# A decoder layer's down product as seven block products, with sums of weights in small chunks on GpSimd and norms on VectorE and ScalarE

## The chip, the cores and the metric

The kernel runs on one core of a Trainium2 chip. The metric is the device time of one execution in microseconds (us). A core has five engines that run side by side and meet through semaphores: TensorE (PE in the rows; PEld is its weight load), VectorE (DVE), ScalarE (ACT), GpSimd (POOL) and SyncE (SP), which here issues every DMA. Each engine takes its instructions strictly in order, and so does SP: a DMA whose semaphores are not there yet holds back all DMAs behind it.

## What is computed

One decoder layer in float32, sequence 1024, width 1024: a mixing layer (dilated attention and a convolution branch), a layer norm, a gated feed-forward network (FFN) of 2816 features, and a second layer norm. The change touches the second half:

```python
ALPHA = 2 ** 0.25
h = silu(x @ w_gate) * (x @ w_up)          # (1024, 2816)
out = layer_norm(ALPHA * x + h @ w_down)   # (1024, 1024)
```

## The kernel before

Every float32 product is three matmuls of rounded halves: `split` (L65, L66) makes a high part by a copy on ACT and a low part by a subtraction on DVE, and `three` pairs them as hi·hi, hi·lo, lo·hi. A matmul has 512 columns and 128 rows of weights. Splits of weights go to five slots of 128x1024.

The FFN runs 22 blocks of 128 features (loop `f`). Each holds seven products, of 12 matmuls each (four slices of the contraction by three), in this order, by the names in the code: B11 and T2 (banks `pa`, `pb`), B21 (again `pa`), T3 (`pd`), T1 (`pc`), T4 (again `pd`), B22 (again `pc`). It is a two-by-two block scheme with seven instead of eight products: the weight sums T1 to T4 are made on DVE (class `Weights`, steps `first` to `fifth`) from two raw units of 512 KB, gate `g` and up `u`, which SP fetches into a pool of three buffers. The next block's steps are written between this block's products. DVE takes each bank out of PSUM with an add (L984, L993, L998, L1000, L1007), since T4 adds onto the bank that T3's add has read. The finished `h` tile of 128x1024 is stored to DRAM (`hd`, L1011), one store per block. The first three blocks (`NEARLY`) have their B11 and B21 products earlier, ahead of the loop.

The down stage is the plain product. For each half `p` of the rows it runs over 22 feature blocks, and for each loads a weight unit (512 KB) and half an `h` tile (256 KB), splits both, and issues 4 row tiles x 2 column halves x 3 = 24 matmuls (L1081) into eight banks. The eight row tiles get `ALPHA * x` from ACT (L1074), then a norm: for seven of them `layer_norm_act`, which gives 640 of 1024 columns of two elementwise steps (L785, L786) to GpSimd and 384 to DVE; for the last one `layer_norm` on DVE, with statistics taken by `bn_stats` (L1056, L1057). Behind the last matmul stand both halves of that last row tile.

The Tile framework's scheduler puts each engine's instructions in order when the kernel is built, so that the order in the code isn't the order on an engine; pools give buffers round robin, and a load into a buffer waits for its last reader.

## Time and profile before

| what | us |
|---|---|
| time before, median of 3 runs | 1659.48 |
| the runs | 1657.36 to 1659.85 |
| the profiled execution's own time | 1657.62 |
| its span (first to last instruction) | 1655.8 |
| PE busy | 1631.6 |
| VectorE busy | 993.4 |
| ScalarE busy | 686.4 |
| GpSimd busy | 47.8 |

The page of the profile gives busy times per engine, then 40 slices of the span, the DMA queues, the chain of work that ended last, the costliest groups of instructions, and DMA issues. "L921 PE" is the engine PE at line 921. A row of a timeline gives start, duration, engine, line, operation, output and inputs by the program's names, shape, count, and in square brackets the idle time ahead of it with what ended it. In the chain of waits a row is one piece of the path that ended last: start, duration, engine and bank. The FFN loop ends at about 1401 us, the down stage's matmuls run from 1404 to 1643 us, and the tail behind them up to 1655.8.

### The profile page before, as it was taken

To read this page: it belongs to the slowest core of one execution; us is meant where nothing else is said; L and a number is where in the kernel's file an instruction comes from. 1 tells how busy PE (TensorE), PEld (TensorE's weight loads), DVE (VectorE), ACT (ScalarE), POOL (GpSimd) and SP (SyncE) were. 2 spreads that over 40 slices of the span, in tenths; PEclk is the share of its full clock that TensorE was granted. 3 is DMA by queue.
4 is the path that set the end of the run, shared out by engine and by line. 5 is a ranking of instruction groups with operands and counts; after the bars stand their busy time and mean duration, and the time that the engine had idled before them with its cause. 6 is when DMAs were issued, how large, how long until landed. Compare 5 with 4: busy or idle time off the path is not lost.

```text
span 1655.8 us, 21072 instructions
## 1 busy us (share of the span) xinstructions
PE 1631.6 (99%) x8146; PEld 1333.3 (81%) x8146; DVE 993.4 (60%) x1599; ACT 686.4 (41%) x1263; POOL 47.8 (3%) x30
## 2 busy tenths in 40 slices
...
GB/s 261 60 43 52 45 52 159 51 46 39 74 153 52 52 77 131 132 252 168 287 92 216 51 77 76 83 95 91 77 76 77 90 89 190 273 146 141 203 89 52
DMA packets 70457, 185.02 MB, mean 112 GB/s; under 512 B 11324, under 2 KB 14652, under 8 KB 70356
## 3 DMA queue, kind: packets, MB, share of 16 engines
...
q14 instruction: 37, 0.30, 0.1%
...
## 4 chain that ended last, share of the span: by engine, by line
PE 93%; DVE 4%; ACT 1%; DMA 1%; issue 1%; DVEq 0%; SPq 0%; ACTq 0%
PE mm L176 43%; PE mm L921 9%; PE s L921 7%; PE t L921 7%; PE mm L1081 5%; PE s L176 4%; PE t L1081 3%; PE s L1081 3%; PE s L414 2%; PE pv L921 2%; PE pv L460 2%; PE pv L1081 2%; PE t L434 1%; PE mm L304 1%; PE pv L176 1%
## 5 line engine op out<-in xcount | busy, mean ns | idle before, releaser
L65 ACT ACTIVATE wh<-raw 128x1024 fp32r<-128x1024 f32 (+1 forms) x206 | 206.5, 1003 | 366.9 <-PE mm L176 83.1
L66 DVE TENSOR_TENSOR wl<-raw,wh 128x1024 fp32r<-128x1024 f32 (+1 forms) x206 | 239.7, 1165 | 192.1 <-ACT wh L65 191.1
L176 PE MATMUL mm<-xh,wh 128*128 128x512 f32 x752 | 298.6, 397 | 0.0
L176 PE MATMUL mm<-xl,wh 128*128 128x512 f32 x752 | 293.2, 390 | 0.0
L176 PE MATMUL mm<-xh,wl 128*128 128x512 f32 x752 | 293.2, 390 | 0.0
L176 PEld LDWEIGHTS mm<-xh,wh 128*128 128x128 f32 x752 | 141.1, 188 | 39.3 <-issue 9.9
L176 PEld LDWEIGHTS mm<-xh,wl 128*128 128x128 f32 x752 | 141.2, 188 | 29.9
L176 PEld LDWEIGHTS mm<-xl,wh 128*128 128x128 f32 x752 | 141.2, 188 | 27.8
L504 DVE SCALAR_TENSOR_TENSOR acc<-u,cp,acc 128x1024 f32<-128x1024 f32 x120 | 153.8, 1282 | 3.3
L347 ACT ACTIVATE sw<-mm 32x512 f32<-32x512 f32 x192 | 113.2, 589 | 35.7 <-PE mm L176 17.3
L66 DVE TENSOR_TENSOR xl<-t,xl 128x512 fp32r<-128x512 f32 x44 | 30.2, 691 | 104.1 <-ACT xl L65 100.8
L176 PE MATMUL mm<-wh,xh 128*128 128x512 f32 x232 | 91.5, 394 | 0.0
L1081 PE MATMUL mm<-wh,xl 128*128 128x512 f32 x264 | 88.5, 389 | 2.4 <-ACT xl L65 2.4
L176 PE MATMUL mm<-wh,xl 128*128 128x512 f32 x232 | 90.4, 390 | 0.0
L176 PE MATMUL mm<-wl,xh 128*128 128x512 f32 x232 | 90.3, 389 | 0.0
L349 DVE TENSOR_TENSOR tcs<-mm,cosF 128x512 f32<-128x512 f32 x48 | 33.1, 690 | 86.0 <-ACT sw L347 82.7
L65 ACT ACTIVATE xl<-t 128x512 fp32r<-128x512 f32 x44 | 27.4, 628 | 122.3 <-PE t L1081 118.8
L378 DVE CUSTOM_DVE_ANT_0 pt<-s,m2t 128x256 f32<-128x256 f32 (+1 forms) x128 | 41.3, 378 | 35.4 <-PE s L414 35.4
L1081 PE MATMUL s<-wh,xl 128*128 128x512 f32 x176 | 61.8, 389 | 0.0
L380 ACT ACTIVATE pt<-pt,stp 128x64 f32<-128x64 f32 (+2 forms) x128 | 49.9, 392 | 27.1 <-DVE stp L378 26.9
L1081 PE MATMUL t<-wh,xl 128*128 128x512 f32 x176 | 60.8, 389 | 0.0
L1081 PEld LDWEIGHTS mm<-wh,xl 128*128 128x128 f32 x264 | 49.6, 188 | 13.1 <-ACT xl L65 2.8
...
## 6 DMA issues: line engine op xcount, KB each, us to landing
raw<-wst SPq DMA_DIRECT2D x165, 512.0 KB, 3.3
hd<-h SPq DMA_DIRECT2D x22, 512.0 KB, 2.6
t<-hd SPq DMA_DIRECT2D x44, 256.0 KB, 3.4
gd<-gt SPq DMA_DIRECT2D x16, 512.0 KB, 3.6
m<-gd SPq DMA_DIRECT2D x32, 256.0 KB, 5.1
...
m<-pvd SPq DMA_DIRECT2D x24, 256.0 KB, 4.7
pvd<-pvs SPq DMA_DIRECT2D x16, 256.0 KB, 2.0
```

The source lines that it names most:

```text
L65: act.activation(hi, src, AF.Copy)
L66: dve.tensor_sub(lo, src, hi.bitcast(F32))
L176: pe.matmul(ps, a, b, start=j == 0, stop=j == n - 1)
L347: act.activation(sw[32 * q:32 * q + 32, :], ps[32 * (q ^ 1):32 * (q ^ 1) + 32, :], AF.Copy)
L349: dve.tensor_mul(tcs, ps, cosF[:, cols])
L378: dve.tensor_tensor_reduce(out=pt, in0=s, in1=msk, scale=-0.125, scalar=BIG, op0=ALU.add, op1=ALU.min, accum_out=mneg)
L380: act.activation(pt, pt, AF.Exp, bias=mneg, scale=-1.0, accum_out=den)
L414: pe.matmul(o, q[rows, i * P:(i + 1) * P], keys(k, i)[rows], start=True, stop=True)
L460: pe.matmul(pv[64 * hh:64 * hh + 64, :], V[g, keys[kb]][:, hd * 64:hd * 64 + 64], pT[:, hh * nb + kb, :], start=kb == 0, stop=kb == nb - 1)
L504: dve.scalar_tensor_tensor(acc, u[:, j:j + S], cp[:, c, j:j + 1], acc, op0=ALU.mult, op1=ALU.add)
L921: pe.matmul(ps, a, b, start=start and n == 0, stop=stop and n == 11, skip_group_check=True)
L1081: pe.matmul(banks[i][c], a, b, start=f == 0 and j == 0, stop=f == NFF - 1 and j == 2)
```

## The change

The down product becomes a seven-product block scheme as well, as in the FFN. The 1024 rows of `h` are cut in two halves of 512 and its 2816 features in two halves of 11 blocks (`NK`); A11, A12 and A22 are blocks of `h` that are stored as they are, and S1 to S4 are sums of blocks that GpSimd makes in place after every second feature block (`down_sums`, four adds of 128x512, then four stores of 256 KB). The FFN takes its feature blocks in pairs k, k + 11 (`FFN_ORDER`), so that the blocks of a pair are at hand together. The sums of `w_down` are made during the FFN as well: `down_weights` takes 22 chunks of [128, 4, 256], two loads of 256 KB each into a pool called `stage`, four subtractions or adds of 128x256 on GpSimd, two stores of 256 KB to DRAM (`twd`); they are named `tw` in the rows of order. The down stage is then a list `DOWN` of seven products of 11 blocks x 4 row tiles x 3 matmuls, 924 matmuls in place of 1056. Each step loads two pieces of 256 KB into the two halves of one 1024 wide tile, splits it at once, and issues 12 matmuls; splits run two steps ahead, loads five further, and six splits of the last product are made earlier and kept in slots of their own. Row tiles 4 to 7 are finished and normed during P2, tiles 0 to 3 in P3, whose four row tiles run one after the other. Behind the last matmul stands one half of one row tile.

The norms leave GpSimd and become two 1024 wide operations on DVE, with the square sum on ACT; the last tile keeps `bn_stats`. Raw units of `u` get two buffers of their own (`up2`), so that `g` has the pool of three alone, and fetches run one unit further ahead. In the FFN `second` moves behind the T1 product, `third` behind T4, `fourth` behind the store of `h`. In the last FFN block the first loads and splits of the down stage take the place of the next block's weights. Whole FFN matmuls, their number and their banks stay as they are.

```diff
-NTAIL = 4
+NK = 11
+FFN_ORDER = [k + NK * c for k in range(NK) for c in range(2)]
...
 
     def fetch(upto):
         while state["raw"] < min(upto, n_units):
             u = state["raw"]
-            t = wraw.tile([P, 1024], F32, tag="raw", name="raw")
+            t = unit_pool[0](u).tile([P, 1024], F32, tag="raw", name="raw")
...
             split(u, *w)
             self.T3, self.T1 = slot_halves(w)
-            fetch(taken[0] + 3)
+            fetch(taken[0] + 4)
...
     p4 = ExitStack()
-    gt8 = p4.enter_context(tc.tile_pool(name="gt8", bufs=8, reuse_waits="tile"))
-    h3 = p4.enter_context(tc.tile_pool(name="h3", bufs=3, reuse_waits="tile"))
+    gt6 = p4.enter_context(tc.tile_pool(name="gt6", bufs=6, reuse_waits="tile"))
+    h4 = p4.enter_context(tc.tile_pool(name="h4", bufs=4, reuse_waits="tile"))
+    up2 = p4.enter_context(tc.tile_pool(name="up2", bufs=2, reuse_waits="tile"))
+    unit_pool[0] = lambda u: up2 if u >= first_pair and (u - first_pair) % 2 else wraw
 
...
+    def row_tile():
+        return h4.tile([P, S], F32, tag="h", name="h")
+
+    def spill_sums(k, u, v):
+
+        for name, src in (("S2", u[:, LEFT]), ("S3", u[:, RIGHT]), ("S4", v[:, LEFT]), ("S1", v[:, RIGHT])):
+            sp.dma_start(hd[name][k], src)
+
+    def down_sums(k, u, v):
+
+        eng = nc.gpsimd
+        eng.tensor_add(v[:, RIGHT], v[:, RIGHT], u[:, RIGHT])
+        eng.tensor_sub(u[:, RIGHT], u[:, LEFT], u[:, RIGHT])
+        eng.tensor_sub(u[:, LEFT], v[:, RIGHT], u[:, LEFT])
+        eng.tensor_sub(v[:, LEFT], v[:, LEFT], u[:, LEFT])
+        after.append(lambda: spill_sums(k, u, v))
+
+    def down_weights(k, e):
+
+        t = stage.tile([P, 4, 256], F32, tag="sp", name="tw")
+        cols = slice(e * 256, (e + 1) * 256)
+
+        def rows(src, n):
+            return src[n].rearrange("p (c x) -> p c x", c=2)[:, :, cols]
+
+        sp.dma_start(t[:, 0:2], rows(wst, n_units + k))
+        sp.dma_start(t[:, 2:4], rows(wst, n_units + NK + k))
+        b11, b12, b21, b22 = (t[:, n] for n in range(4))
+        eng = nc.gpsimd
+        eng.tensor_sub(b12, b22, b12)
+        eng.tensor_add(b11, b12, b11)
+        eng.tensor_sub(b21, b21, b11)
+        eng.tensor_sub(b22, b22, b11)
+
+        def spill():
+            sp.dma_start(rows(twd, k), t[:, 0:2])
+            sp.dma_start(rows(twd, NK + k), t[:, 2:4])
+        after.append(spill)
+
+    chunks = deque((k, e) for k in range(NK) for e in range(2))
+
+
+    DOWN = [("P1", "A11", (0, 0), 0, True), ("P6", "S2", (2, 0), 1, True), ("P7", "S3", (2, 1), 0, True),
+            ("P5", "S1", (3, 1), 1, True), ("P4", "A22", (3, 0), 0, False), ("P2", "A12", (1, 0), 0, True),
+            ("P3", "S4", (1, 1), 1, False)]
...
+    for j in range(len(DOWN)):
+        for k in range(NK):
+            if (j, k) not in seq:
...
+    def split_upto(key, ahead):
+        upto = min(seq.index(key) + 1 + ahead, len(seq))
+        while dpos[1] < upto:
+            j, k = seq[dpos[1]]
+            load_upto(dpos[1] + 1)
+            w = kept[k] if j == len(DOWN) - 1 and k < len(kept) else slot()
+            split(draw.pop((j, k)), *w)
+            dsplit[j, k] = w
+            dpos[1] += 1
+            load_upto(dpos[1] + 5)
...
     for f in range(NFF):
         last = f == NFF - 1
+        todo, after = after, []
+        for fn in todo:
+            fn()
+        if f >= NEARLY:
+            for _ in range(2 if f in (5, 9, 13) else 1):
+                if chunks:
+                    down_weights(*chunks.popleft())
         V_, W = W, Weights()
...
-        if nxt:
-            nxt.second()
         u3, sg2 = half_tile(), half_tile()
...
         dve.tensor_add(u3, u2, pd)
-        if nxt:
-            nxt.third()
...
+        if nxt:
+            nxt.second()
         product(pd, V_.T4, a22, start=False)
...
         if nxt:
-            nxt.fourth()
+            nxt.third()
         else:
...
+        k = FFN_ORDER[f] % NK
+        if f % 2 == 0:
+            sp.dma_start(hd["A11"][k], ht[:, LEFT])
+            hrows.append(ht)
+        else:
+            sp.dma_start(hd["A12"][k], ht[:, LEFT])
+            sp.dma_start(hd["A22"][k], ht[:, RIGHT])
+            down_sums(k, hrows.pop(), ht)
         if nxt:
+            nxt.fourth()
             nxt.fifth()
...
+    def norm(i):
+        y = yt[i // 4][:, i % 4]
         sc = sc2[:, i]
-        for c in range(2):
-            yc = y[:, c * HALF:(c + 1) * HALF]
-            if i < 7:
...
+        if i == 3:
+            layer_norm(y, bs2, mv2, sc, g2, b2, HALF, emit_rows(i))
+            return
+        nmu, ssq, v, sd, r, t = (sc[:, n:n + 1] for n in range(2, 8))
+        dve.tensor_scalar(nmu, sc[:, 0:1], sc[:, 1:2], -1.0 / D, op0=ALU.add, op1=ALU.mult)
+        act.activation(junk, y, AF.Square, bias=nmu, accum_out=ssq)
+        act.activation(sd, ssq, AF.Sqrt, bias=eps, scale=1.0 / D)
+        dve.scalar_tensor_tensor(y, y, nmu, g2, op0=ALU.add, op1=ALU.mult)
+        dve.tensor_scalar(v, ssq, 1.0 / D, LN_EPS, op0=ALU.mult, op1=ALU.add)
+        rsqrt_of(v, sd, r, t)
+        dve.scalar_tensor_tensor(y, y, r, b2, op0=ALU.mult, op1=ALU.add)
+        emit_rows(i)(slice(0, D))
...
+    def after_product(name, i, ps):
+        if name == "P1":
+            act.activation(u2(i), ps, AF.Copy)
+            scaled(i, 0, u2(i))
+        elif name == "P6":
+            dve.tensor_add(u2(i), u2(i), ps)
+        elif name == "P7":
+            dve.tensor_add(u3(i), u2(i), ps)
+            scaled(4 + i, 0, u2(i))
+            scaled(i, 1, u2(i))
+            scaled(4 + i, 1, u3(i))
+        elif name == "P5":
+            add_in(4 + i, 1, ps)
+        elif name == "P4":
+            add_in(4 + i, 0, ps)
+        elif name == "P2":
+            add_in(i, 0, ps)
         else:
...
+    def loads():
+        for i in (0, 1, 2, 3, 4, 5, 6, 7):
+            sp.dma_start(yt[i // 4][:, i % 4], yd[i])
+            yield
+        ln_rows(1, g2, b2)
+        yield
+
...
+    for j, (name, _, _, sset, first) in enumerate(DOWN):
+        if first:
+            banks[sset] = [bank(t) for t in sets[sset]]
+        last = j == len(DOWN) - 1
...
+                pe.matmul(banks[sset][i], a, b, start=first and k == 0 and m == 0,
+                          stop=k == NK - 1 and m == 2, skip_group_check=True)
+
+        if not last:
+            for k in range(NK):
+                split_upto((j, k), 2)
+                for i in range(4):
+                    step(i, k)
+                    if k == NK - 1:
+                        after_product(name, i, banks[sset][i])
+                if k % 2 == 0:
+                    next(fill, None)
+                if name == "P2" and k in (1, 3, 5, 7):
+                    norm(4 + k // 2)
...
             for i in range(4):
...
+                for k in range(NK):
+                    if i == 0:
+                        split_upto((j, k), min(2, NK - 1 - k))
+                    step(i, k)
+                after_product(name, i, banks[sset][i])
+                norm(i)
```

Order on SyncE before, at the ends of feature blocks 4 to 6: `hd` is the store of a block's `h`, `raw` the fetches of two units for later blocks.

```order
L1011 DMA hd4_99<-h_8623 128x1024 [waits DVE_49]
L77 DMA raw_8760<-wst 128x1024 [waits DMAHW7_49,DVE_49,Activation_49]
L77 DMA raw_8762<-wst 128x1024 [waits DMAHW5_49,DMAHW1_49,DVE_49]
L1011 DMA hd5_100<-h_8751 128x1024 [waits DVE_49]
L77 DMA raw_8888<-wst 128x1024 [waits DMAHW2_49,DVE_49,Activation_49]
L77 DMA raw_8890<-wst 128x1024 [waits DMAHW4_49,DMAHW0_49,DVE_49]
L1011 DMA hd6_101<-h_8879 128x1024 [waits DVE_49]
L77 DMA raw_9016<-wst 128x1024 [waits DMAHW5_49,DVE_49,Activation_49]
L77 DMA raw_9018<-wst 128x1024 [waits DMAHW7_49,DMAHW3_49,DVE_49]
```

One store and two fetches stand there per block, and nothing between them waits for GpSimd. After, SyncE in the same part of the FFN; `tw` rows are loads of chunks and `twd` rows their stores, `raw_8897` is a unit of `g` and `raw_8750` a unit of `u`, `hdA11_2` a store of `h`.

```order
L979 DMA tw_9621<-wst 128x2x256 [waits DMAHW4_49]
L978 DMA tw_9767<-wst 128x2x256 [waits DMAHW5_49,DMAHW0_49]
L988 DMA twd4_176<-tw_9484 256x1x256 [waits DMAHW6_49,DMAHW1_49,Pool_49]
L989 DMA twd15_187<-tw_9484 256x1x256 [waits DMAHW7_49,DMAHW2_49,Pool_49]
L988 DMA twd5_177<-tw_9621 256x1x256 [waits DMAHW3_49,Pool_49]
L81 DMA raw_8897<-wst 128x1024 [waits DVE_49,Activation_49]
L989 DMA twd16_188<-tw_9621 256x1x256 [waits DMAHW4_49,Pool_49]
L979 DMA tw_9767<-wst 128x2x256
L81 DMA raw_8750<-wst 128x1024 [waits DVE_49]
L1094 DMA hdA11_2_97<-h_8735 128x512 [waits DMAHW5_49,DVE_49]
L988 DMA twd5_177<-tw_9767 256x1x256 [waits DMAHW6_49,Pool_49]
L989 DMA twd16_188<-tw_9767 256x1x256 [waits DMAHW7_49,DMAHW3_49,Pool_49]
```

The fetches of `raw` now stand behind stores that wait for GpSimd (Pool in the waits). Some four chunks stand in the queue per FFN block there, not one, since the scheduler has moved them up: all 22 are out ahead of the store of block 8 (counted from 0). Between the fetches of the `u` units for blocks 5 and 9 stand the loads and stores of 16 chunks and of two groups of sums of `h`.

VectorE before, from the end of one block into the next: L894 is the first subtraction of weights on a unit `u` of a later block, L1007, L1009 and L1010 finish this block's `h`, L984 and L993 take banks `pb` and `pd` out.

```order
L894 TENSOR_TENSOR raw_8888<-raw_8888 128x512 [waits DMAHW7_49]
L1007 TENSOR_TENSOR t_8764<-t_8764,mm2_8834 128x512 [waits DVE_49,PE_49]
L66 TENSOR_TENSOR wl_8909<-raw_8762,wh_8908 128x1024 [waits DMAHW5_49,Activation_49]
L1009 TENSOR_TENSOR h_8879<-t_8765,t_8764 128x512 [waits DVE_49]
L895 TENSOR_TENSOR raw_8762<-raw_8888,raw_8762 128x512 [waits DVE_49]
L899 TENSOR_TENSOR raw_8762<-raw_8762 128x512 [waits DVE_49]
L984 TENSOR_TENSOR t_8892<-t_8892,pv_8912 128x512 [waits PE_49,Activation_49]
L66 TENSOR_TENSOR wl_8959<-raw_8762,wh_8958 128x1024 [waits PE_49,Activation_49]
L993 TENSOR_TENSOR t_8941<-t_8892,t1_8943 128x512 [waits DVE_49,PE_49]
```

The unit `raw_8888` that L894 reads was fetched a block earlier. After, VectorE in a block: L880 is that same first subtraction, now of a unit for the block after next, L1065, L1072 and L1077 take out `pb`, `pd` and `pc`, and L69 is the subtraction of a split.

```order
L69 TENSOR_TENSOR wl_8933<-raw_8748,wh_8932 128x1024 [waits DMAHW3_49,Activation_49]
L881 TENSOR_TENSOR raw_8748<-raw_8750,raw_8748 128x512 [waits DVE_49]
L885 TENSOR_TENSOR raw_8748<-raw_8748 128x512 [waits DVE_49]
L880 TENSOR_TENSOR raw_8899<-raw_8899 128x512 [waits DMAHW3_49]
L1065 TENSOR_TENSOR t_8916<-t_8916,mm1_8936 128x512 [waits PE_49,Activation_49]
L69 TENSOR_TENSOR wl_9011<-raw_8748,wh_9010 128x1024 [waits PE_49,Activation_49]
L1072 TENSOR_TENSOR t_8963<-t_8916,s0_8965 128x512 [waits DVE_49,PE_49]
L1077 TENSOR_TENSOR t_8963<-t_8963,mm2_8979 128x512 [waits DVE_49,PE_49]
```

L880 with its wait for a fetch (`raw_8899`) now stands ahead of L1065 and L1072 of the block that is running.

GpSimd after, in the same part: four adds on `h` tiles for the sums, then chunks.

```order
L964 TENSOR_TENSOR h_8589<-h_8589,h_8454 128x512 [waits DMAHW0_49,DVE_49]
L965 TENSOR_TENSOR h_8454<-h_8454 128x512 [waits PE_49,Pool_49]
L966 TENSOR_TENSOR h_8454<-h_8589,h_8454 128x512 [waits Pool_49]
L967 TENSOR_TENSOR h_8589<-h_8589,h_8454 128x512 [waits DMAHW7_49,DVE_49,Pool_49]
L982 TENSOR_TENSOR tw_9484<-tw_9484 128x256 [waits DMAHW4_49,DMAHW2_49,DMAHW1_49]
L983 TENSOR_TENSOR tw_9484<-tw_9484 128x256 [waits Pool_49]
L984 TENSOR_TENSOR tw_9484<-tw_9484 128x256 [waits Pool_49]
L985 TENSOR_TENSOR tw_9484<-tw_9484 128x256
L982 TENSOR_TENSOR tw_9621<-tw_9621 128x256 [waits DMAHW4_49,DMAHW3_49]
```

Before, GpSimd had nothing to do in the FFN blocks; now sums of `h` and chunks share its one queue.

## Rows read from the trace of the kernel before

**Rows 1.** The page: span, and engines' busy time, share of span, instructions.

```profile
span 1655.8 us, 21072 instructions
PE 1631.6 (99%) x8146; PEld 1333.3 (81%) x8146; DVE 993.4 (60%) x1599; ACT 686.4 (41%) x1263; POOL 47.8 (3%) x30
```

**Rows 2.** Chain of waits: start, us, engine, bank, line, count; one FFN, one down piece.

```profile
1352.39 10.88 PE t L921 x48
...
1425.77 2.04 PE mm L1081 x9
```

**Rows 3.** Timeline of PE: the first matmul of the down stage and the last.

```profile
1403.71 0.50 PE L1081 MATMUL mm<-wh,xl 128*128 128x512 f32 x1 [2.37 <-ACT xl L65]
...
1642.98 0.39 PE L1081 MATMUL t<-wh,xl 128*128 128x512 f32 x1
```

**Rows 4.** Timeline of VectorE behind the last matmul.

```profile
1644.26 1.28 DVE L1056 TENSOR_TENSOR xh<-xh,t 128x512 f32<-128x512 f32 x2
...
1647.94 0.68 DVE L1057 BATCH_NORM_STATS2 xl<-xh 128x6 f32<-128x512 f32 x1
```

**Rows 5.** Windows: stretch, length, busy (count) of PE, PEld, DVE, ACT, POOL; PEclk, DMA share, GB/s.

```profile
964.00:968.00 4.00, 0.41 (x4) 0.17 (x2) 3.36 (x6) 1.48 (x3) 0.00 (x0) 1.00 0.30 119
968.00:972.00 4.00, 3.79 (x15) 2.81 (x16) 4.00 (x9) 2.93 (x7) 0.72 (x1) 0.63 0.01 4
1134.00:1210.00 76.00, 76.00 (x337) 62.94 (x336) 45.21 (x61) 21.70 (x28) 0.00 (x0) 1.00 0.24 83
1400.00:1520.00 120.00, 117.64 (x519) 97.07 (x519) 46.31 (x53) 44.69 (x56) 0.00 (x0) 1.00 0.58 198
```

**Rows 6.** Timeline of GpSimd: adds of 128x512, and of 128x640 in the norms.

```profile
943.86 1.30 POOL L813 TENSOR_TENSOR y<-y 128x512 f32<-128x512 f32 x1
...
946.60 2.15 POOL L815 TENSOR_TENSOR y<-y 128x512 f32<-128x512 f32 x1
...
1530.20 1.95 POOL L785 TENSOR_TENSOR xh<-xh,xl 128x640 f32<-128x640 f32 x1 [552.08 <-ACT xh L780]
```

**Rows 7.** Timeline of VectorE while GpSimd was busy, 941 to 948 us.

```profile
941.37 1.26 DVE L766 SCALAR_TENSOR_TENSOR y<-y,mv,lng 128x1024 f32<-128x1024 f32 x1
942.55 1.24 DVE L616 SCALAR_TENSOR_TENSOR sc<-sc 128x1 f32<-128x1 f32 x1
...
945.21 2.40 DVE L767 SCALAR_TENSOR_TENSOR y<-y,sc,lnb 128x1024 f32<-128x1024 f32 x1
947.53 0.68 DVE L837 SCALAR_TENSOR_TENSOR y<-y,mm 128x512 f32<-128x512 f32 x1
```

**Rows 8.** Timeline of VectorE in one steady FFN block.

```profile
1187.11 0.69 DVE L66 TENSOR_TENSOR wl<-raw,wh 128x512 fp32r<-128x512 f32 x1
...
1195.49 0.69 DVE L899 TENSOR_TENSOR raw<-raw 128x512 f32<-128x512 f32 x1
...
1197.45 0.69 DVE L984 TENSOR_TENSOR t<-t,pv 128x512 f32<-128x512 f32 x1 [1.26 <-PE pv L921]
...
1201.02 1.22 DVE L66 TENSOR_TENSOR wl<-raw,wh 128x1024 fp32r<-128x1024 f32 x1 [2.88 <-ACT wh L65]
```

**Rows 9.** The page's groups: the two halves of a split; busy, mean ns.

```profile
L65 ACT ACTIVATE wh<-raw 128x1024 fp32r<-128x1024 f32 (+1 forms) x206 | 206.5, 1003 | 366.9 <-PE mm L176 83.1
L66 DVE TENSOR_TENSOR wl<-raw,wh 128x1024 fp32r<-128x1024 f32 (+1 forms) x206 | 239.7, 1165 | 192.1 <-ACT wh L65 191.1
```

**Rows 10.** The page's DMA issues: count, KB each, median us to landing.

```profile
raw<-wst SPq DMA_DIRECT2D x165, 512.0 KB, 3.3
t<-hd SPq DMA_DIRECT2D x44, 256.0 KB, 3.4
```

**Rows 11.** Timeline of SyncE's own queue in the FFN: issue times.

```profile
1112.42 3.09 SPq L77 DMA_DIRECT2D raw<-wst  x2
...
1118.72 0.33 SPq L1011 DMA_DIRECT2D hd<-h  x1
```

**Rows 12.** Timeline of ScalarE in a norm: the square sum.

```profile
1628.07 1.15 ACT L775 ACTIVATE xl<-xh,xl 128x1024 f32<-128x1024 f32 x1 [6.02 <-DVE xl L774]
```

165 lines of the change are left out of this document (71 added, 94 removed).

## The prediction

> **What bounds the kernel now.** I read the page first: PE is busy 1631.6 of 1655.8 us, no other engine above 60% [rows 1]. Then the chain of waits over the FFN and the down stage: nearly every piece is TensorE, 48 matmuls in 10.88 us and nine in 2.04 us, so 0.2267 us each in both stages [rows 2]; the 0.39 us in a timeline row is the pipelined length, of which only the spacing counts [rows 3]. The windows say the same: in 1134 to 1210 us PE is busy all 76.00 us while VectorE has 45.21, ScalarE 21.70 and GpSimd nothing [rows 5]. So a matmul less is worth 0.2267 us, and any other work costs nothing until it makes TensorE wait. The reader should therefore look for two things: matmuls that go, and new work that TensorE comes to wait for. Only two stretches here are not TensorE's: 2.37 us ahead of the first down matmul, and the tail from the last matmul, which starts at 1642.98, to the end of the span at 1655.8 [rows 1, 3].
>
> **The change part by part.** *Matmuls.* The down product goes from 1056 to 924 matmuls: 132 x 0.2267 = 29.9 us gone, if the rest keeps up.
>
> *Hand-over into the down stage.* TensorE waits 2.37 us there for the first split of `h` [rows 3]. After the change the first loads and splits stand in the last FFN block, ahead of its last product, and a block gives 84 x 0.2267 = 19.04 us of cover: −2.4. Without the cover the same 2.4 us return, no more.
>
> *Tail.* From the last matmul's end, 1642.98 + 0.39 = 1643.37, to 1655.8 are 12.4 us now, with two adds and two statistics of the last tile and a norm of the tile before it mixed in. Afterwards one half is added (0.64, two took 1.28), its statistics are taken, and the rest of that norm runs as now: from the second statistics at 1647.94 to the end are 7.9 us [rows 4]. With 0.15 to start, 8.7 us: −3.7. The gains sum to 36.0 us.
>
> *Down stage, cover of the rest.* A step lasts 12 x 0.2267 = 2.72 us and holds one split, 1.003 us of ScalarE and 1.165 of VectorE [rows 9], and two loads of 256 KB: 512 KB in 2.72 us is 193 GB/s, and the window over the present down stage shows 198 GB/s at a DMA share of 0.58 [rows 5]. Over the stage VectorE has 77 splits (90 us), about 44 adds of 0.69 (30 us) and eight norms of about 3.5 us, two 1024 wide operations of 1.26 [rows 7] and small ones: about 148 us in 77 x 2.72 = 209 us. ScalarE adds eight square sums of 1.15 us [rows 12]. On average this is hidden. The tightest place is P2, where four norms and four adds meet the splits: I count 23 to 24 us of VectorE's queue ahead of a split that is needed 27.2 us later. I take 0 there and keep 0 to 6 us (one split and its norm late in each of two steps) for the range. GpSimd gives up its 640 columns, which lie on no path but the tail.
>
> *Sums on GpSimd, and the queue of SyncE.* This is the term that decides. The trace has GpSimd idle in the FFN; 88 operations of 128x256 and 44 of 128x512 come in. Their own time would hide, but each chunk's store waits for GpSimd, the next chunk's load is queued behind that store, and the fetches of the raw units `g` and `u` are queued behind both on SyncE. VectorE in turn holds L880, which reads the fetched unit `u`, in its in-order queue ahead of L1065 and L1072, the adds that free banks; TensorE's T4 product, 5 x 2.72 = 13.6 us into a block, adds onto the bank that L1072 reads. From the landing of `u` to L1072's end stand three operations like L899 and L984 (0.69) and one 1.22 split [rows 8], 3.3 us, and a unit lands 3.3 us after its issue [rows 10]. So a fetch that leaves SyncE later than 13.6 − 3.3 − 3.3 = 7.0 us into the block makes TensorE wait, one for one. Now nothing like this can happen: one store (0.33 us) and two fetches per block, and no wait on GpSimd [rows 11].
>
> How long does SyncE take? Between the fetch of `u` for block 5 and that for block 9, four blocks or 76.2 us of TensorE, it has to pass 16 chunks, two groups of sums of `h`, and about eight places (counted in the order) where GpSimd has nothing loaded: T = 16c + 2s + 8e.
>  - c, four operations of 128x256. A 128x512 one takes 1.30 alone [rows 6], half is 0.65, with 0.07 to the next. VectorE and GpSimd get in each other's way: an add took 2.15 instead of 1.30 [rows 6], a VectorE operation on one column 1.24, and a 1024 wide one 2.40 where its like took 1.26; but an add that reads PSUM took its usual 0.68 beside GpSimd [rows 7]. In an FFN block ten VectorE operations have two inputs in SBUF, 8.5 us of 19.04 (three of 1.22, seven of 0.69; [rows 8] has the first and the last of them). So 44% of GpSimd's operations meet one and wait half of its 0.85: 0.19 each. c = 4 x (0.65 + 0.07 + 0.19) = 3.6. Low: no waits, 2.9. High: a 256 wide operation no shorter than a 512 wide one, 4 x 1.36 = 5.4. The 128x640 row, 1.95, scales to 0.78 per 256 [rows 6], so I stay near the low half.
>  - s, four of 128x512: 4 x (1.30 + 0.07 + 0.19) = 6.2; 5.5 without waits, 7.2 with half of them at 2.15.
>  - e, one store's issue 0.33 and a load of 256 KB, 3.4 to its landing [rows 10, 11]: 3.7; low 2.7 (the load at 2.4), high 4.1 (two issues).
>
> T = 57.6 + 12.4 + 29.6 = 99.6 us, 23.4 over the cover. Block 3 begins about 4 us late by the same count, with the first chunks ahead of its fetches: **27 us of stall**. A second count that needs no queue: GpSimd's bare operations in these blocks are 16 x 2.6 + 2 x 5.2 = 52 us and VectorE's two-input ones 4 x 8.5 = 34; if they exclude each other, 86 us must fit into 76, so some 10 us are lost even with loads that never lag. Later blocks have no chunks and nothing gives the loss back, as TensorE is full. After TensorE has stood for long, its clock costs more: at 964 to 968 us it was busy 0.41 us of 4 and in the next 4 us the granted clock was 0.63 [rows 5], some 1.5 us of work lost; I add 1.5 once. Ends: T = 46.4 + 11.0 + 21.6 = 79 gives 7 us of stall, T = 86.4 + 14.4 + 32.8 = 134 gives 61.
>
> *Sum*, on the profiled execution's 1657.62 us: −36.0 + 27 + 1.5 = 1650.1. That execution is 1.9 us below the median of the runs (1659.48), so **1652** as a median.
>
> **A rule on the other side of c.** The rows show 1.30 us for 128x512 on GpSimd [rows 6] and 0.69 for the same on VectorE [rows 8]. The Trainium skill (GPSIMD Engine Reference, section "Engine selection") says to keep such adds on VectorE and off GpSimd, as about twice as slow, which the two rows bear out (1.9 times); by the rule the chunks belong on VectorE, where 88 adds of half of 0.69 would take some 30 us of its spare time and no SyncE wait on GpSimd would be left. Its section "Elementwise — side-by-side cycle accounting" gives about 2.6 cycles per element, by which I estimate 0.56 us for 256 columns; with that c is 2.5 without waits and the sum ends as in the first rival below.
>
> **The rivals.**
>  - *The chunk loop hides.* If VectorE and GpSimd seldom meet, c is 2.9, and if loads of the next chunk mostly run beside the one at work, e counts in five places or fewer: T = 46.4 + 11.0 + 18.5 = 76, no more than the cover, the fetches leave in time, and stalls stay at 0 to 10 us. Then 1657.6 − 36.0 + 4 + 1.9 = 1628. For it: GpSimd's rate alone, and a `u` pool with two buffers that lets fetches run ahead. Against it: the exclusion in [rows 6, 7] and the 86 us count.
>  - *The chunk loop costs more than the matmuls give: slower.* At 5.4 us per chunk (fixed cost per operation dominating, so that 256 columns cost 1.29), T = 86.4 + 12.4 + 29.6 = 128.4; the stall is 56 us and the time 1657.6 − 36.0 + 56 + 1.5 + 1.9 = 1681. It decides against the kernel from c = 4.25, about 1.06 us per operation with its wait: there 4 + (68 + 12.4 + 29.6 − 76.2) = 38 us of stall eat the 36. For it: the adds shown are 512 wide or wider, and one took 2.15 [rows 6]; nothing in the trace is 256 wide. Against it: 640 columns cost more than 512, so columns do count.
>  - *The down stage doesn't keep its spacing.* Splits, adds and norms share VectorE in P2, banks pass from P4 to P2 through four adds, and the loads need 193 GB/s without a break. If a third of the 77 steps lose 1 us beside the forecast's stall, the time is 1652 + 26 = 1678; with no stall in the FFN it is 1654. For it: loads with no spare buffers ahead of a norm. Against it: VectorE is needed for only 148 of 209 us.
>
> **How the numbers follow.** Forecast (stall of 15 to 38 us, 1640 to 1663): 0.40. Chunk loop hidden, about 1628: 0.25. Chunk loop slower than that, 1664 to 1690: 0.25. Down stage: 0.10, spread over 1640 to 1680. A measurement of this kernel can tell about 0.2%, 3.3 us, so no change is 1656.2 to 1662.8. Faster: 0.27 of the forecast's 0.40, all of the first rival and 0.02 of the last, 0.54. Same: 0.10 and 0.03, 0.13. Slower: 0.03, 0.25 and 0.05, 0.33. The range takes in the first rival to 1626 and two thirds of the second, to 1680. The forecast's own is 1640 to 1663.
>
> **What would show it.** In the profile after: about 132 matmuls fewer, and the down stage's steps at 2.72 us; TensorE gaps at T4 in FFN blocks 3 to 8 with L1072 or L880 behind them, and SyncE's queue waiting on GpSimd ahead of them; blocks from 9 on at 19.04 us; GpSimd operations of 256 columns at 0.65 to 0.9 us; no gap ahead of the first down matmul; the tail at 8.7 us. GpSimd operations above 1 us mean the second rival, blocks at 19.04 throughout the first. A down stage above 209.5 us between its first and last matmul means the third. Wrong altogether would be the model if TensorE stalls in blocks that have no chunks.

## The result, and the profile after

The changed kernel takes 1671.35 us (median of 5 runs; four lie between 1669.85 and 1671.49, one at 1679.55) against 1659.48 before: a ratio of 1.008, 95% interval 1.0054 to 1.0106. It is 12 us slower. The profiled execution took 1669.85 us, its span is 1668.0.

The first rows are the page of the kernel after (span; PE's busy time; busy tenths of GpSimd and tenths of TensorE's clock in 40 slices of 41.7 us):

```profile
span 1668.0 us, 21325 instructions
PE 1614.5 (97%) x8014; PEld 1316.0 (79%) x8014; DVE 1034.5 (62%) x1605; ACT 684.9 (41%) x1241; POOL 161.9 (10%) x148
...
POOL 0000000000000000000000223555411112100000
PEclk9999999999999999999999999978999999999999
```

TensorE is busy 17 us less than in [rows 1], but the span is 12.2 longer, and its clock falls in the slices in which GpSimd works most. Next, TensorE's timeline: the first matmul of the FFN (of the products that stand ahead of the loop), the five matmuls ahead of which it waited over 1 us in the FFN blocks that have chunks, the last of the FFN and the first of the down stage, and the last matmul.

```profile
969.71 0.50 PE L907 MATMUL mm<-xh,wh 128*128 128x512 f32 x1 [3.70 <-ACT xh L785]
...
1060.19 0.80 PE L907 MATMUL t<-a22h,wh 128*128 128x512 f32 x1 [5.45 <-DVE t L1072]
...
1089.85 0.79 PE L907 MATMUL s<-a22h,wh 128*128 128x512 f32 x1 [7.43 <-DVE t L1072]
...
1118.30 0.79 PE L907 MATMUL t<-a22h,wh 128*128 128x512 f32 x1 [7.35 <-DVE t L1072]
...
1149.93 0.80 PE L907 MATMUL s<-a22h,wh 128*128 128x512 f32 x1 [9.48 <-DVE t L1072]
...
1176.08 0.80 PE L907 MATMUL t<-a22h,wh 128*128 128x512 f32 x1 [4.42 <-DVE t L1072]
...
1449.35 0.39 PE L907 MATMUL t<-s24h,wl 128*128 128x512 f32 x1
1449.57 0.39 PE L1201 MATMUL mm<-wh 128*128 128x512 f32 x1
...
1659.40 0.39 PE L1201 MATMUL t<-wh,wl 128*128 128x512 f32 x1
```

The same two ends of the FFN in the kernel before:

```profile
968.11 0.50 PE L921 MATMUL mm<-xh,wh 128*128 128x512 f32 x1 [3.71 <-ACT xh L801]
...
1400.96 0.39 PE L921 MATMUL t<-s24h,wl 128*128 128x512 f32 x1
```

Set beside [rows 3], this is the account of the change; the FFN ends where its last matmul starts.

| stretch | before | after | difference |
|---|---|---|---|
| start to the last FFN matmul | 1400.96 | 1449.35 | +48.39 |
| to the first down matmul | 2.75 | 0.22 | −2.53 |
| to the last down matmul | 239.27 | 209.83 | −29.44 |
| to the end of the span | 12.82 | 8.60 | −4.22 |
| span | 1655.8 | 1668.0 | +12.2 |

All the gains that were forecast are there. The loss up to the last FFN matmul is 48.4 us. Of this, 1.6 us are there already at the first FFN matmul (969.71 against 968.11), 47 us ahead of the first load of a chunk, so they aren't the chunks' (kernels that are alike up to there differ by as much, see "L880 later"). The rest lies where the forecast put it: five waits, 34.1 us in all, each at the first matmul of T4 (`a22h,wh`), each for L1072.

One of these waits, the fourth, from the SyncE queue to TensorE (three timelines; on SyncE a row is the issue):

```profile
1134.23 0.56 SPq L988 DMA_DIRECT2D twd<-tw  x1
...
1138.77 0.51 SPq L989 DMA_DIRECT2D twd<-tw  x1
1139.99 0.44 SPq L81 DMA_DIRECT2D raw<-wst  x1
...
1145.49 1.58 DVE L880 TENSOR_TENSOR raw<-raw 128x512 f32<-128x512 f32 x1 [14.21 <-DMA raw<-wst]
...
1147.00 0.68 DVE L1065 TENSOR_TENSOR t<-t,mm 128x512 f32<-128x512 f32 x1
...
1149.20 0.67 DVE L1072 TENSOR_TENSOR t<-t,s 128x512 f32<-128x512 f32 x1
```

Four stores of sums (L988, L989; the first and the last are shown) wait one by one for GpSimd, the fetch of `u` goes out behind them at 1139.99 (the unit `raw` of the row), VectorE stands at L880 for 14.21 us until the unit is there, and L1065 and L1072 follow; TensorE starts 0.06 us after L1072's end. That is the chain of the prediction, link by link. Over the whole stretch of four blocks, 1051 to 1169 us, SyncE waits 49.9 us for GpSimd's chunk adds (L982 to L985) ahead of the stores, and 13.0 us for its sums of `h`.

### The profile page after: what moved, and what is told of

It reads as the page before. It is cut to its first block, busy times and chain, and to the rows that moved or that the text cites. A ratio compares the mean times of both kernels' runs of the same rounds, so it can differ in the third digit from the quotient of the medians.

```text
span 1668.0 us, 21325 instructions
## 1 busy us (share of the span) xinstructions
PE 1614.5 (97%) x8014; PEld 1316.0 (79%) x8014; DVE 1034.5 (62%) x1605; ACT 684.9 (41%) x1241; POOL 161.9 (10%) x148
## 3 DMA queue, kind: packets, MB, share of 16 engines
q1 hardware_dynamic: 110708, 221.17, 39.4%
## 5 line engine op out<-in xcount | busy, mean ns | idle before, releaser
L68 ACT ACTIVATE wh<-raw 128x1024 fp32r<-128x1024 f32 (+1 forms) x192 | 192.4, 1002 | 442.2 <-PE mm L180 83.1
L69 DVE TENSOR_TENSOR wl<-raw,wh 128x1024 fp32r<-128x1024 f32 (+1 forms) x192 | 227.9, 1188 | 184.8 <-ACT wh L68 183.5
L180 PE MATMUL mm<-xh,wh 128*128 128x512 f32 x752 | 298.5, 397 | 0.0
L180 PE MATMUL mm<-xl,wh 128*128 128x512 f32 x752 | 293.2, 390 | 0.0
L180 PEld LDWEIGHTS mm<-xh,wl 128*128 128x128 f32 x752 | 141.2, 188 | 29.9
L351 ACT ACTIVATE sw<-mm 32x512 f32<-32x512 f32 x192 | 113.3, 590 | 34.9 <-PE mm L180 16.5
L796 POOL TENSOR_TENSOR y<-y 128x512 f32<-128x512 f32 x3 | 6.5, 2167 | 956.9 <-DVE sc L618 947.6
L180 PE MATMUL mm<-wh,xl 128*128 128x512 f32 x232 | 90.4, 390 | 0.0
L69 DVE TENSOR_TENSOR wl<-h,wh 128x1024 fp32r<-128x1024 f32 x41 | 50.6, 1235 | 33.7 <-ACT wh L68 32.1
L68 ACT ACTIVATE wh<-h 128x1024 fp32r<-128x1024 f32 x41 | 43.5, 1061 | 63.7 <-PE s L1201 26.4
L384 ACT ACTIVATE pt<-pt,stp 128x64 f32<-128x64 f32 (+2 forms) x128 | 49.9, 392 | 27.1 <-DVE stp L382 26.9
L907 PE MATMUL mm<-xh,wh 128*128 128x512 f32 x140 | 55.5, 398 | 4.4 <-ACT xh L785 4.4
L880 DVE TENSOR_TENSOR raw<-raw 128x512 f32<-128x512 f32 x22 | 16.6, 755 | 63.4 <-DMA raw<-wst 63.4
L907 PE MATMUL mm<-xl,wh 128*128 128x512 f32 x140 | 55.4, 396 | 0.0
```

The costliest lines, as they stand in the source:

```text
L68: act.activation(hi, src, AF.Copy)
L69: dve.tensor_sub(lo, src, hi.bitcast(F32))
L180: pe.matmul(ps, a, b, start=j == 0, stop=j == n - 1)
L351: act.activation(sw[32 * q:32 * q + 32, :], ps[32 * (q ^ 1):32 * (q ^ 1) + 32, :], AF.Copy)
L384: act.activation(pt, pt, AF.Exp, bias=mneg, scale=-1.0, accum_out=den)
L796: eng.tensor_add(v[:, RIGHT], v[:, RIGHT], v[:, LEFT])
```

## Experiments

Twelve kernels ran. The kernel before took 1659.03 to 1659.96 us as the median beside them. In the table, "over no_chunks" is what the chunks cost in each variant.

| run | median us | over no_chunks | ratio to before (95%) |
|---|---|---|---|
| no_chunks | 1620.49 | 0 | 0.9767 (0.9751 to 0.9783) |
| gated (one chunk per block) | 1622.64 | 2.2 | 0.9773 (0.9756 to 0.979) |
| gated_late_l880 | 1622.88 | 2.4 | 0.9781 (0.9767 to 0.9796) |
| two_per_block | 1638.0 | 17.5 | 0.9862 (0.9845 to 0.9878) |
| no_adds | 1639.83 | 19.3 | 0.9879 (0.9861 to 0.9897) |
| adds_on_vectore | 1642.89 | 22.4 | 0.9897 (0.9882 to 0.9912) |
| three_per_block | 1650.89 | 30.4 | 0.9941 (0.9926 to 0.9956) |
| late_l880 | 1655.02 | 34.5 | 0.997 (0.9956 to 0.9984) |
| contiguous_chunks | 1666.31 | 45.8 | 1.0043 (1.003 to 1.0056) |
| the changed kernel (about four per block) | 1671.35 | 50.9 | 1.008 (1.0054 to 1.0106) |
| fetch_on_scalare | 1679.71 | 59.2 | 1.0109 (1.0089 to 1.013) |
| chunks_on_gpsimd_queue | 1803.51 | 183.0 | 1.0872 (1.0854 to 1.089) |
| norms_alone (from the kernel before) | 1657.46 | | 0.9988 (0.9978 to 0.9997) |

### Without the chunks

```diff
             for _ in range(2 if f in (5, 9, 13) else 1):
-                if chunks:
-                    down_weights(*chunks.popleft())
+                pass
...
-            b = wst[n_units + kind * NK + k] if kind < 2 else twd[(kind - 2) * NK + k]
+            b = wst[n_units + (kind % 2) * NK + k]
```

> The 22 chunks of weight sums are left out whole (their loads, adds and stores), and the down stage reads raw w_down units in place of the sums, so the number of loads and matmuls of the down stage stays. In the changed kernel TensorE left the FFN loop 48.5 us later than in the kernel before (last FFN matmul at 1449.5 against 1401.0 us). Queue theory (the chunks' loads and stores on SyncE hold back the fetches of u): all of it goes, 1671.4 - 48.5 = 1623, 1621 to 1627. Rival, the sums of h on GpSimd and their stores cost a part of it: 1630 to 1650. Rival, the new order of the steps on VectorE is what stalls TensorE (L880 ahead of L1065 and L1072): it stays near 1671.

1620.49 us, 0.5 us below the expected range. The window over the FFN loop shows TensorE busy without a break (columns as in [rows 5]):

```profile
998.00:1400.00 402.00, 402.00 (x1778) 332.85 (x1777) 250.82 (x318) 114.41 (x145) 56.08 (x40) 1.00 0.33 112
```

So the chunks are the whole loss; the sums of `h`, their 44 stores and the new order on VectorE, all still in this run, cost nothing that shows. It also gives the gains alone: 1659.86 − 1620.49 = 39.4 us by the medians, 1655.8 − 1618.2 = 37.6 by the spans, where the prediction summed 36.0.

### One chunk per block

```diff
-            sp.dma_start(hd["A11"][k], ht[:, LEFT])
+            stored = sp.dma_start(hd["A11"][k], ht[:, LEFT])
...
-            sp.dma_start(hd["A22"][k], ht[:, RIGHT])
+            stored = sp.dma_start(hd["A22"][k], ht[:, RIGHT])
...
                 if chunks:
-                    down_weights(*chunks.popleft())
+                    with tc.issue_after(stored.ins if hasattr(stored, "ins") else stored):
+                        down_weights(*chunks.popleft())
```

> Nothing is left out. The loads of a block's chunk are queued on SyncE behind the store of the block before (an order of issue, no wait), so that one or two chunks stand in each of 18 blocks instead of four in each of four or five. Queue theory: 19 us of cover per block against about 3.6 us of adds, 3 of sums of h and one or two exposed loads of 4 to 5 us: the fetches leave in time, 1622 to 1630, faster than the kernel before by 2%. Rival, position on VectorE (L880 ahead of L1065 and L1072 makes TensorE wait for any late unit): each block still waits for its chunk, 3 us and more in each of 18 blocks, 1650 to 1680.

1622.64 us: the same adds, loads and stores, one order more, and 49 us less. This is 2.3% less than the kernel before and beats both. SyncE's queue over a little more than a block:

```profile
1098.11 0.33 SPq L1099 DMA_DIRECT2D hdA<-h  x1
...
1099.92 0.60 SPq L978 DMA_DIRECT2D tw<-wst  x1
...
1103.90 4.43 SPq L959 DMA_DIRECT2D hdS<-h  x4
1110.51 0.57 SPq L988 DMA_DIRECT2D twd<-tw  x1
...
1113.80 3.09 SPq L81 DMA_DIRECT2D raw<-wst  x2
```

The chunk's two loads (L978, L979) go out behind the store of `h`, its stores (L988, L989) 10 us later, and the two fetches go out in 3.09 us just as in [rows 11]. The rival that L880's place alone makes TensorE wait falls, since L880 stands where it stood, ahead of the adds that take the banks out, and TensorE is busy for all of 998 to 1400 us:

```profile
998.00:1400.00 402.00, 402.00 (x1772) 332.89 (x1771) 252.17 (x318) 113.75 (x146) 131.08 (x128) 1.00 0.50 166
```

### Two and three per block

```diff
-            for _ in range(2 if f in (5, 9, 13) else 1):
+            for _ in range(2):
```

(3 in the other run, both with the order of gated.)

> As in the run gated, nothing left out, but two chunks per FFN block, in blocks 3 to 13. Queue theory, a rate: two chunks are about 7 us of adds, 3 of sums of h, one exposed load of 4 to 5 and about 3 of issues, 17 to 18 us against a cover of 19.04 per block: nearly nothing is lost, 1622 to 1632. Rival, any chunk that is queued ahead of a fetch delays it, rate or not: the loss is twice that of one per block and more, 1635 to 1650.

> Three chunks per FFN block, in blocks 3 to 10. Queue theory, a rate: 11 us of adds, 3 of sums, two exposed loads of 4 to 5 and 5 of issues, 22 to 25 us against 19.04, so 3 to 6 us are lost in each of about seven blocks: 1640 to 1665, between the changed kernel (four per block, 1671) and two per block. Rival, only the moved L880 and not the number matters: as gated, about 1623.

1638.0 and 1650.89 us. The second is as expected. The first is a miss: 17.5 us are lost where 17 to 18 us of work per block should have fitted into 19.04. SyncE's timeline shows why, fetches of two blocks and what stands between:

```profile
1096.74 1.05 SPq L81 DMA_DIRECT2D raw<-wst  x2
...
1105.29 5.30 SPq L959 DMA_DIRECT2D hdS<-h  x4
1110.63 1.32 SPq L978 DMA_DIRECT2D tw<-wst  x1
...
1122.06 1.04 SPq L81 DMA_DIRECT2D raw<-wst  x2
...
1138.56 1.05 SPq L81 DMA_DIRECT2D raw<-wst  x2
```

From fetch to fetch are 25.3 us in the block with sums of `h` and 16.5 in the one without, 41.8 for two blocks against 38.1 of TensorE's. In the first, one thing waits for the other: the store of `h`, the four adds on `h`, their stores (L959, 5.30 us), the second chunk's loads (1110.63), its adds, its stores, and only then the fetch. My estimate had averaged the sums over blocks and let them run beside the loads. So the rate decides, as the queue theory has it, but the work is a chain more than I had counted. From one chunk to the hoisted four the cost rises in steps of 15, 13 and 21 us.

### L880 later

```diff
-        dve.tensor_add(u3, u3, pc)
+        taken_out = dve.tensor_add(u3, u3, pc)
         if nxt:
-            nxt.second()
+            with tc.issue_after(taken_out.ins if hasattr(taken_out, "ins") else taken_out):
+                nxt.second()
```

> Nothing is left out. The first subtraction on a unit u (L880) is queued on VectorE behind the add L1077 of the block ahead of the one that needs it, where the code has it, and no longer a block earlier; the chunks stay where they were on SyncE. Queue theory (a rate: SyncE needs 117 us where TensorE gives 76.2): the later deadline gives about 26 us of slack once and no rate, so 20 to 25 us of the 48.5 stay, 1643 to 1650. Rival, position: with L1072 no longer behind L880 TensorE does not wait, 1622 to 1628. If the slack is worth nothing: 1671.

1655.02 us, above the 1643 to 1650 of the queue theory and far from the 1622 to 1628 of the rival: 16 us are won, not 26, and not all. TensorE no longer waits for L1072; the waits have moved to split weights and to the first bank's copy on ScalarE. VectorE and TensorE around the longest but one:

```profile
1121.54 0.69 DVE L880 TENSOR_TENSOR raw<-raw 128x512 f32<-128x512 f32 x1 [8.08 <-DMA raw<-wst]
...
1123.60 0.68 DVE L1082 TENSOR_TENSOR t<-t,s 128x512 f32<-128x512 f32 x1
...
1124.88 0.59 PE L907 MATMUL pv<-s24h,wh 128*128 128x512 f32 x1 [3.99 <-ACT wh L68]
...
1132.39 0.80 PE L907 MATMUL s<-xh,wh 128*128 128x512 f32 x1 [2.57 <-ACT t L1060]
```

L880 again stands 8.08 us for the unit, now with L1082 and the split of the next block's weights behind it. So the later deadline is worth 16 us here and leaves the queue as slow as it was. With one chunk per block it is worth nothing:

> gated and late_l880 together, nothing left out. If the 2.1 us between gated (1622.6) and no_chunks (1620.5) are waits for a unit u, the later L880 takes them: 1620 to 1622. In late_l880 TensorE waited at other places instead, for split weights and for ScalarE's copy of the first bank; if the later steps are too late even with one chunk per block: 1625 to 1640.

1622.88 us, no different from gated. The 2 us that gated keeps over no_chunks aren't waits for a unit `u`, and in the profiled executions they aren't the chunks' at all. In gated the first FFN matmul starts at 969.53 us, in no_chunks at 967.46, long before gated's first load of a chunk at 1042.8; from there to the end of the span are 651.3 and 650.8 us, and TensorE is busy for all of 998 to 1400 us in both. (In gated_late_l880 it waits 2.6 us there, for split weights.) Ahead of the FFN the kernels are the same. In 786 to 794 us, around the same wait of 1.45 us, the granted clock is 0.93 in gated and 1.00 in no_chunks. The twelve profiled kernels with the seven-product down stage (the changed one and its variants) start the FFN between 967.2 and 969.9 us, so a difference of 2 us in the table says nothing of the chunks.

### The adds left out, and the adds on VectorE

```diff
-        eng = nc.gpsimd
-        eng.tensor_sub(b12, b22, b12)
-        eng.tensor_add(b11, b12, b11)
-        eng.tensor_sub(b21, b21, b11)
-        eng.tensor_sub(b22, b22, b11)
```

(in the second run `eng = dve`, and the adds stay)

> The chunks are loaded and stored as they are; only their four GpSimd operations are left out (the down stage then multiplies raw weights). Queue theory: SyncE still has to pass 16 chunks of four DMAs at about 0.6 us each between the fetches of u for blocks 5 and 9, and each store still waits for a load to land (4.2 us), so T falls from 117 to about 85 to 95 us and some 10 to 25 us of loss stay: 1633 to 1648. Rival, GpSimd's adds and VectorE's two-input operations shutting each other out are the loss: without the adds nearly all of it goes, 1622 to 1628.

> The four adds of each chunk run on VectorE in place of GpSimd, chunks otherwise hoisted as before, four per block, stores and fetches on SyncE. VectorE has 0.35 to 0.4 us per add, 88 adds or 33 us. Queue theory: between no_adds (1640) and the changed kernel (1671), since loads and issues stay and the adds are half as long but stand in VectorE's order: 1640 to 1665. Rival, the loss is GpSimd's slow adds and its meeting VectorE: no more than no_adds, 1622 to 1640.

1639.83 and 1642.89 us. The first is where the queue theory put it, and its rival falls. Of the 50.9 us some 19 stay when the chunks are only loaded and stored, so GpSimd's adds, with all that they hold up, are about 31.5, and the traffic in SyncE's queue the rest. On VectorE the same 88 adds cost 3 us more than none, though each took 0.49 to 0.57 us there on average, not the 0.35 to 0.4 that I had expected (GpSimd took 0.79 to 0.90 in the stretch shown below). The second run doesn't separate the two theories, since 1642.9 lies just outside what the rival allowed and near the lower end of the other. It does bear out the rule of the Trainium skill (GPSIMD Engine Reference, section "Engine selection") that elementwise adds belong on VectorE: at the same place in the order that is worth 28 us here. The page's other section, "Elementwise — side-by-side cycle accounting", gave 0.56 us for 256 columns as an estimate in the prediction; the kernel after has 0.74 for an add that nothing disturbed (one row of GpSimd's timeline), and the measurement decides:

```profile
1053.41 0.74 POOL L983 TENSOR_TENSOR tw<-tw 128x256 f32<-128x256 f32 x1
```

### The fetches on ScalarE's queue

```diff
-            sp.dma_start(t, wst[u])
+            (act if u >= unit_q[0] else sp).dma_start(t, wst[u])
```

(`unit_q[0]` is the first unit of the FFN pairs.)

> The chunks stay where the changed kernel has them, four per block on SyncE; only the fetches of the raw units g and u of the FFN pairs are issued from ScalarE's queue, so that no store that waits for GpSimd stands ahead of them. Queue theory (the fetches lose their time behind those waits, and nothing else is short): 1621 to 1630. Rival, GpSimd, VectorE and the DMA engines are overfull in these blocks whatever the queue: 1640 to 1671. A cost of its own: ScalarE may now stand in front of a fetch whose buffer is not free and hold back splits, up to 20 us.

1679.71 us, slower than the changed kernel: neither 1621 to 1630 nor the rival as it was meant. ScalarE's timeline shows two fetches, and what ScalarE waited for ahead of the work behind each:

```profile
1076.48 0.33 ACTq L82 DMA_DIRECT2D raw<-wst  x1
1076.86 0.63 ACT L1084 ACTIVATE t<-t 128x512 f32<-128x512 f32 x1 [13.48 <-DMA tw<-wst]
...
1087.48 0.33 ACTq L82 DMA_DIRECT2D raw<-wst  x1
1087.86 0.60 ACT L1062 ACTIVATE t<-mm 128x512 f32<-128x512 f32 x1 [8.47 <-DMA twd<-tw]
```

The fetches wait for a chunk's DMA (the idle times of 13.48 and 8.47 us end with a load `tw<-wst` and a store `twd<-tw`), though no data connects them. In the order of the instructions a fetch has such a wait (here the next two fetches):

```
L82 DMA raw_8897<-wst 128x1024 [waits DMAHW1_49,DVE_49,Activation_49]
L1084 ACTIVATE t_8672<-t_8672 128x512 [waits DVE_49]
L68 ACTIVATE wh_8744<-raw_8469 128x1024 [waits PE_49]
L68 ACTIVATE wh_8784<-raw_8607 128x1024 [waits PE_49]
L82 DMA raw_8750<-wst 128x1024 [waits DMAHW0_49,DVE_49]
```

`DMAHW1` is one of eight such names, 0 to 7, in the orders of this kernel and of the changed one: semaphores that the program gives to the DMAs of SyncE and ScalarE in turn, so that a DMA waits for the one that had its semaphore before it. The first fetch in this order waits for the count that a chunk's load gives `DMAHW1`, the second for one that another chunk's load gives `DMAHW0`. As the chunks' DMAs take part in that turn, the fetch is tied to them on either of these two queues. ScalarE's copies of the first bank (L1062) stood behind it, and TensorE waited 47 us for these. So this run does not test a free queue.

### The chunks' DMAs on GpSimd's queue

```diff
-        sp.dma_start(t[:, 0:2], rows(wst, n_units + k))
+        nc.gpsimd.dma_start(t[:, 0:2], rows(wst, n_units + k))
```

(and the same for the second load and both stores)

> The chunks' loads and stores are issued from GpSimd's own queue, with semaphores of their own, ahead of and behind its adds; nothing of them stands on SyncE any more, and the chunks are hoisted as before. (In fetch_on_scalare the fetches still waited on a semaphore lane that a chunk's DMA had used last, so that they were no freer than on SyncE.) Queue theory: the fetches leave in time though GpSimd does the same adds at the same place: 1621 to 1632. Rival, adds on GpSimd and the DMA traffic are too much for these blocks themselves: 1640 to 1671. Third outcome: GpSimd needs so long to issue its DMAs that the sums of h come late and SyncE waits for these, 1630 to 1660.

1803.51 us: the third outcome in kind, but far beyond the 1660 that I had allowed for it. GpSimd's timeline (DMA rows are its own issues), and TensorE's waits, 990 to 1600 us:

```profile
1081.72 0.74 POOL L978 DMA_DIRECT2D tw<-wst  x1 [4.27 <-issue]
1085.45 0.74 POOL L979 DMA_DIRECT2D tw<-wst  x1 [2.99 <-issue]
```

```profile
PE t L907 <- DVE t L1072: 170.9, 4, 82.8
```

An issue takes GpSimd 0.7 us in the row and another 1 to 4 idle ahead of it: loads with nothing between them stand 3.4 to 3.8 us apart. 88 loads and stores make the sums of `h` late, and SyncE still holds their stores ahead of the fetches: TensorE waits 170.9 us. Whether a queue that is wholly free, for these chunks at this density, would have hidden them stays open: neither run made one.

### Longer runs of memory

```diff
-            return src[n].rearrange("p (c x) -> p c x", c=2)[:, :, cols]
+            return src[n][:, e * HALF:(e + 1) * HALF].rearrange("p (c x) -> p c x", c=2)
```

> The changed kernel with one thing different: a chunk's loads and stores read and write one run of 512 columns (2 KB) per partition in place of two runs of 256 (1 KB each), the same bytes, adds and order; so it sums columns that do not belong together. In the changed kernel a chunk's DMA takes 0.51 to 0.63 us to issue and 4.2 to land, where a whole run of 512 columns took 0.33 to issue and 3.2 to 3.6 to land. If the small pieces cause the term that the prediction sized too low (about ten gaps of GpSimd of 4.6 us each in place of 3.7, and half of SyncE's issue time): 10 to 16 us less than the changed kernel, 1655 to 1662. If landing is slow because of the traffic as a whole: 0 to 5 us less, 1666 to 1671.

1666.31 us, 5 us less than the changed kernel and so in the second of the two ranges, at its lower end (ratio 1.0043 against 1.008, with intervals that just meet). SyncE's timeline, one issue, and the DMA issues with the median landing of the chunks' loads:

```profile
1055.24 0.33 SPq L978 DMA_DIRECT2D tw<-wst  x1
```

```profile
tw<-wst SPq DMA_DIRECT2D x44, 256.0 KB, 4.2
```

The issue falls from 0.6 to 0.33 to 0.44 us, so that part is the piece size; the landing stays at 4.2. The 5 us that went aren't clear in the one profile, which happened to be of a run near the upper end (span 1667.1). So the 1 KB pieces aren't what makes the loads land late. The traffic as a whole doesn't explain it either. In gated the DMA share in 998 to 1400 us is 0.50, not the 0.66 of the changed kernel's stretch with chunks (below), and a chunk's load still takes 4.0 us:

```profile
tw<-wst SPq DMA_DIRECT2D x44, 256.0 KB, 4.0
```

The load `t<-hd` of the kernel before took 3.4 us [rows 10] in a stage with a share of 0.58 [rows 5], and with two chunks per block a chunk's load took 5.6 at the same 0.58 (1050 to 1290 us). What sets the landing time stays open.

### The norms alone

The kernel before with `norm`'s two VectorE operations in place of `layer_norm_act`'s rest.

```diff
+        dve.scalar_tensor_tensor(y, y, nmu, g, op0=ALU.add, op1=ALU.mult)
...
-        dve.tensor_mul(t, nmu, r)
-        act.activation(y, y, AF.Identity, bias=t, scale=r)
...
-            for eng, cs in ((nc.gpsimd, slice(cut, D)), (dve, slice(0, cut))):
-                eng.tensor_mul(y[:, cs], y[:, cs], g[:, cs])
-                eng.tensor_add(y[:, cs], y[:, cs], b[:, cs])
...
+            dve.scalar_tensor_tensor(y, y, r, b, op0=ALU.mult, op1=ALU.add)
```

> The kernel before with one part of the change alone: the seven norms run on VectorE and ScalarE without GpSimd, two 1024 wide operations of VectorE; the last tile and the plain down product stay. Theory of the prediction: behind the last matmul both halves of the last row tile stay, so nearly all of the 12.4 us stays, and the gain of 3.7 comes from the order of the row tiles: 1657 to 1661, no change. Rival, GpSimd's part of the norm before is what the tail waits for: 2 to 4 us less, 1655 to 1657.

1657.46 us (ten runs), 0.03% to 0.22% less: inside what the prediction calls no change, and at the border of the two expectations, so the time alone doesn't decide. The trace tells more. TensorE's last matmul, in a span of 1655.6 us:

```profile
1644.98 0.39 PE L1076 MATMUL t<-wh,xl 128*128 128x512 f32 x1
```

From there to the end of the span are 10.6 us, against 12.8 before and 8.6 in the changed kernel. The new form of the norms alone shortens the tail by 2.2 us, the rival's share; the other 2.0 of the 4.2 come with the changed down stage, where one half of a row tile stands behind the last matmul.

## Why the prediction was wrong

The forecast was 1652 us, 0.5% faster; it is 1671, 0.8% slower, inside the range but on the other side of no change. The steps, one by one:

- **Matmuls, hand-over, tail: right in size.** −29.9, −2.4 and −3.7 were forecast, −29.44, −2.53 and −4.22 are measured. For the tail the mechanism is only half right: VectorE has one add of a half behind the last matmul, as forecast (below), but that order gives 2.0 us, and the norms, to which the sum gave no price of their own, give 2.2. That the total came out is partly luck.

```profile
1659.83 0.69 DVE L1133 TENSOR_TENSOR xh<-xh,t 128x512 f32<-128x512 f32 x1 [1.84 <-PE t L1201]
```

- **Down stage hidden: right.** TensorE waited 0.3 us in all of it. The window of its first 60 us has a DMA share of 0.80 and 282 GB/s, more than the 193 of the sum, as loads run five steps ahead, and TensorE stays busy (first row; the other two are read further down):

```profile
1449.00:1509.00 60.00, 60.00 (x267) 49.67 (x266) 32.99 (x31) 25.41 (x26) 6.88 (x4) 1.00 0.80 282
1051.26:1168.33 117.07, 87.36 (x339) 70.05 (x338) 54.74 (x61) 23.29 (x30) 66.86 (x75) 0.85 0.66 215
1060.00:1065.00 5.00, 4.81 (x11) 3.80 (x12) 2.69 (x4) 0.00 (x0) 3.29 (x5) 0.50 0.53 173
```

- **The mechanism of the loss: right.** SyncE behind GpSimd, L880, L1072, T4, in blocks 3 to 7, none in later ones.
- **T, the time that SyncE needs from the fetch of `u` for block 5 to that for block 9: wrong, and this is the step that failed.** The forecast was 99.6 us, the trace has 1051.26 to 1168.33, 117.1. Its parts, by GpSimd's groups in just that window (busy, mean ns | idle before):

```profile
L983 POOL TENSOR_TENSOR tw<-tw 128x256 f32<-128x256 f32 x16 | 14.4, 898 | 1.3
...
L982 POOL TENSOR_TENSOR tw<-tw 128x256 f32<-128x256 f32 x17 | 13.5, 794 | 43.4 <-DMA tw<-wst 22.7 <-issue 14.8 <-DVE wl L69 5.9
...
L964 POOL TENSOR_TENSOR h<-h 128x512 f32<-128x512 f32 x2 | 3.0, 1486 | 3.8 <-DMA hdA<-h 3.8
```

  *c* and *s* were right: busy time in the window is 66.9 us, with 3.0 in the gaps of about 0.07 between operations 69.9, and 16c + 2s was 70.0 (the window holds 67 chunk adds, a little over 16 chunks). The chunk adds are 0.79 to 0.90 us each by line, waits included, against 0.84 in the sum. *e* was wrong in both factors. GpSimd is idle 43.4 + 3.8 = 47.2 us where 8e was 29.6. There are ten places over 2 us (I had counted eight in the order), 4.6 us each in place of 3.7: two more places are 9.2 us, 0.9 more in each of eight is 7.4, and two short ones are 1.0. In 22.7 of the 43.4 us the profile names a chunk's load as what ended the wait; for the rest it names none, or VectorE, but there too L982 starts 3 to 5 us behind the issue of a load. A load of a chunk lands after 4.2 us, not the 3.4 of [rows 10], and a chunk's store or load mostly takes 0.51 to 0.66 us to issue, not the 0.33 of [rows 11]. The nearest rows were of another stage and of other pieces. The longer issue is the piece size, as the run with longer pieces shows; why the loads land later stays open. A price from one stage, taken for another kind of load, and a count from the order made *e* too low.
- **The lateness of the first block** was put at 4 us. T4 of block 3 begins at 1053.0 us in the kernel before and at 1060.2 after, 7.2 later. Of these, 1.6 were there at the start of the FFN; 5.6 are the block's.
- **The clock: right as a sum, for a reason the prediction didn't give, so in part by luck.** TensorE waited 34.1 us, but left the FFN 48.4 later; 1.6 were there before, and the other 12.7 are the price of matmuls at the lower of the clock's two levels, as in the third row above, 11 matmuls in 5 us at a granted clock of 0.50, after a wait of 5.45 us. Yet that is not to be added five times: T4 begins 29.7, 28.5, 31.6 and 26.2 us apart, 115.9 in all, and the fetches 117.1, so the queue sets the pace and a slow stretch only shortens the next wait. What is left to add is the stretch behind the last wait: 1176.08 to the end of the FFN, 14 x 19.04 + 5.4 = 272.0, took 273.5, that is 1.5, as forecast.

In all: 1.6 ahead of the FFN, 5.6 in block 3, 115.9 − 76.2 = 39.7 in the four that follow, 1.5 of clock, 48.4 us, where 4 + 23.4 + 1.5 had been summed. Most of the miss is T, 17.5 us, and in it *e*, 17.6; the first block adds 1.6.

**The rivals.** Slower was held at 0.33, with the mechanism that an add of 256 columns costs as much as one of 512. That is not what happened (0.74 us alone, against 1.30 in [rows 6]); the places where GpSimd has nothing loaded did it. From c = 4.25 the kernel was to lose; with e at 4.6 in ten places it loses with c = 3.6. The first rival, that the loop hides, describes gated: with one chunk per block and everything else the same, 1622.6, where 1628 had been worked out for it. That the 86 us count gave 10 us of loss even with loads that never lag is neither shown nor refuted: in gated the same work is spread over 18 blocks.
